# A macaron transformer kernel: the input's block sums move into the places of the lead tiles' weights, between the lead tiles' products

## The chip, the cores and the metric

The kernel runs on one core of one Trainium2 chip. The metric is the device time of one execution in microseconds (us), the median over several runs. A core has a matrix engine (TensorE, PE in the profile; PEld are its weight loads), a vector engine (VectorE, DVE), an activation engine (ScalarE, ACT), GpSimd (POOL) and SyncE (SP), which here issues the DMAs. Each engine works through its own queue in order and waits at semaphores for the others.

## What is computed

Two layers act on a latent stream of 512 tokens and a context stream of 256 tokens, width 1024. Each layer is a half-step feed-forward part (FFN), a mixer and a second half-step FFN. There are four FFNs, numbered 0 to 3 here as in the kernel (`fi`); FFN 3 has no context stream.

```python
def swiglu(h, w_gu, w_down):
    gate, up = jnp.split(h @ w_gu, 2, axis=-1)
    return (jax.nn.silu(gate) * up) @ w_down

def macaron_ffn(x, g, shift, scale, gate, w_gu, w_down):
    h = modulate(rms_norm(x, g), shift, scale)
    return x + 0.5 * gate * swiglu(h, w_gu, w_down)
```

The hidden width is 2816, which is 22 tiles of 128 columns.

## The kernel before, in words

**Numbers in two parts.** Every fp32 operand of a product is split into a high part, rounded by ACT (`ACT.copy`), and a low part, the difference, made by DVE. Each product is then three matmuls (`mm3`, lines 296 to 298): high by high, high by low, low by high. `hh` and `hl` hold the two parts of the normed input, eight tiles `kt` of 128 rows by all the tokens.

**An FFN.** Its 22 gate and up tiles come in two ways. The first three are the lead tiles (`lead`, L446): plain products over kt = 0 to 7, once for each of two streams of columns. In FFN 1 and 2 the first stream is the context (256 columns) and the second the latent (512); in FFN 3 they are the two halves of the latent, 256 columns each. The weights of the lead tiles are loaded and split while the stage before still runs (`lead_ffn`, L323): 12 pairs of tiles of 512 columns, 48 KB of each partition. After a stream's products, `activate` (L410) makes silu(gate) times up from PSUM: L414 on ACT, L415 on DVE, L416 on ACT, L417 on DVE, through one buffer `sg`. The other 19 tiles come from `gu_w` (L504), a product scheme with seven block products in place of eight: the input is cut in four blocks (rows TOP and BOT, columns H1 and H2), and the products need four block sums of the input, `tblk[0]` to `tblk[3]`, and sums of the weights (L509 to L514). `gu_w` runs its products in the order w11, s1 on `tblk[0]`, s2 on `tblk[1]`, s4, s3 on `tblk[2]`, w12, w22 on `tblk[3]`. The second of them that writes the bank `ox` (s2) needs the first one's result copied out first (`keep`, L536), into a buffer of the tag `t2`.

**The block sums.** `combos` (L467) makes all four sums once for each FFN, for four k each: DVE subtractions and additions (L479 to L481, for the last sum L501 and L502) into a `tsum` buffer of the tags `nacc` and `t2` (two buffers each), then the high part on ACT (L474) and the low part on DVE (L475). In FFN 1 to 3 it is called after `lead`, when the lead tiles' pool is closed (L571) and a pool for eight tiles of sums is opened in the same 48 KB (32 KB in FFN 3).

**After the lead tiles** come the down products of the first three hidden tiles (`down`, L609; residual at L309), then chunks of `gu_w` and `down` in turn. Weights stand in a ring of 6 slots (8 in FFN 3) filled by `fill` (ACT L317, DVE L318). DVE also makes the modulation rows of later stages (L146) in FFN 0 to 2.

**PSUM.** There are eight banks, four of the tag `ps` and four of `pb`. The second stream of the lead tiles holds six of them in FFN 1 and 2 and three in FFN 3 until `activate` has read them.

**Order.** The order on each engine is no written one: a scheduler sets it when the program is built, by program order and by when its own model has each instruction ready. A tile that takes the place of another waits for all that read the other.

Of the kernel before, what the change touches and what calls it, by code (L numbers as in the profile page):

```python
# [51 lines left out]
def hybrid_backbone_kernel(ctx: ExitStack, tc: tile.TileContext, A: dict, out: bass.AP):  # L52
# [69 lines left out]
    def pump(n=1):  # L122
        for _ in range(n):
            if pending:
                try:
                    next(pending[0])
                except StopIteration:
                    pending.pop(0)
# [194 lines left out]
    def lead_ffn(fi):  # L323

        lp, close = opened("lead%d" % fi, side="right")
        ws = [[tuple(lp.tile([P, 512], F32R, tag=q, name="lead" + q, bufs=12) for q in "hl") for _ in range(4)] for _ in range(3)]

        def load():
            for i in range(3):
                for w, a in zip(ws[i], wload(A["wgl"][fi, i], 2048, 4)):  # L330
                    fill(w, a, LEAD, act_last)
                yield
        return ws, close, load()

    def lead_mixer(src, name):

# [15 lines left out]
    def ffn(l, f, with_ctx, jobs=(), next_sub=None, opening=False, lead_in=None, lead_out=None):  # L352
# [9 lines left out]
        TOP, BOT = slice(0, 4), slice(4, 8)  # L362
        nslot = NSLOT if jobs else 8
        set_psum(f"pf{fi}", "single")
        pool_t = []
        with tc.tile_pool(name=f"ffn{fi}", bufs=1, reuse_waits="tile") as fp:

            def slot():
# [5 lines left out]
            def tt(dt=F32R):  # L374
                return pool_t[0].tile([P, 4 * nh], dt, tag="tt", name="tt", bufs=8)
# [23 lines left out]
            def lead_k(w):  # L399

                return [tuple(tuple(a[:, (kt % 2) * 256 + j * P:(kt % 2) * 256 + j * P + P] for a in w[kt // 2]) for j in range(2)) for kt in range(KT)]

            def act_tiles():
                return [fp.tile([P, T], F32R, tag="a" + q, name="a" + q, bufs=NACT) for q in "hl"]
# [41 lines left out]
            def lead(ws, each=None):  # L446

                acts = acts0
                for c0, n in (LAT, CT) if opening else (CT, LAT) if with_ctx else (LA, LB):
                    if n == S:  # L450
                        drain()
                    bs = [gate_up(n) for _ in ws]
                    for kt in range(KT):
                        if each is not None and n == S:
                            each(kt)
                        for w, b in zip(ws, bs):
                            for j in range(2):
                                down_last[:] = [mmg(b[j], w[kt][j], kt, c0, n, kt == 0 and (j == 0 or n == S), kt == KT - 1 and (j == 1 or n == S))]
                        pump()
                    for act, b in zip(acts, bs):  # L460
                        activate(act, c0, *b)
                drain()
                return acts

            tblk = []
            pe_last, dve_last = [], []

            def combos():

                def tmp(tag):  # L470
                    return sm.tile([P, 512], F32, tag=tag, name="tsum", bufs=2)[:, :nh]

                def done(i, k, t):
                    ACT.copy(tblk[i][0][:, k], t)  # L474
                    return V.tensor_tensor(tblk[i][1][:, k], t, tblk[i][0][:, k], op=ALU.subtract)  # L475

                def sums(e, o, first, *terms):
                    op = ALU.subtract
                    e.tensor_tensor(o, first[0], terms[0][0], op=op)  # L479
                    e.tensor_tensor(o, o, terms[0][1], op=op)  # L480
                    e.tensor_tensor(o, o, first[1], op=ALU.add)  # L481

                ts = [tt().rearrange("p (k c) -> p k c", k=4) for _ in range(8)]
                t1, t3, t2, t4 = (ts[2 * i:2 * i + 2] for i in range(4))
                tblk.extend((t1, t2, t3, t4))
                bl = [[[(hh[:, kt, q], hl[:, kt, q]) for q in (H1, H2)] for kt in (k, k + 4)] for k in range(4)]
                for k in range(4):
                    (b11, b12), (b21, b22) = bl[k]
                    a = tmp("nacc")
                    sums(V, a, b12, b11)  # L490
                    done(0, k, a)
                    b = tmp("t2")
                    sums(V, b, b22, b12)
                    done(2, k, b)
                for k in range(4):
                    (b11, b12), (b21, b22) = bl[k]
                    b = tmp("t2")
                    sums(V, b, b22, [x[:, k] for x in t1])
                    done(1, k, b)
                    a = tmp("nacc")  # L500
                    V.tensor_tensor(a, b21[0], b, op=ALU.subtract)  # L501
                    V.tensor_tensor(a, a, b21[1], op=ALU.add)  # L502
                    dve_last[:] = [done(3, k, a)]

            def gu_w(ft):
                a11, a21, a12, a22 = wload(A["wgs"][fi, ft - 3], 2048, 4)
# [55 lines left out]
            if opening:  # L562
                open_t()
                rows = [tt(F32) for _ in range(4)]
                ws = lead_slots()
                acts0 = [act_tiles() for _ in range(3)]
                queue = start_up(rows, ws, lead_k, fill, lead)
            else:
                acts0 = [act_tiles() for _ in range(3)]
                queue = lead([lead_k(w) for w in lead_in[0]])  # L570
                lead_in[1]()  # L571
                open_t()
            ndirect = NDIRECT[fi]
            if ndirect == 3:
                combos()
            ft = 3

            state = {}
# [15 lines left out]
            for ci, nf in enumerate(CHUNKS[fi > 0]):  # L594
                while len(queue) < nf:
                    queue.append((gu if ft < ndirect else gu_w)(ft))
                    ft += 1
                    if ft == ndirect:
                        combos()
                acts, queue = queue[:nf], queue[nf:]  # L600
                last = ci == len(CHUNKS[fi > 0]) - 1
                norms = {}
                if last:
                    some_jobs(len(jobs))
                if last and next_sub is not None:
                    sqrt_table()
                    sq = cycle([sg_tile()[:, :512], s3_tile()] + job_tiles(fp, 0) + [job_tiles(fp, 1) for _ in range(NWM)])
                    norms = {vec_index(q[0]): Norm(*q, *next_sub, room=lambda: next(sq), tail=TAIL) for q in (LAT, CT)}
                    pool_t[1]()  # L609
                    lead_next = lead_out()  # L610

                def down(dt, w, c0, n):
                    po = bank()
                    for i in range(nf):
                        cs = slice(i * P, i * P + P)
                        with issue_after(pe_last if i == 0 else ()):
                            down_last[:] = [mm3(po[:, :n], w[0][:, cs], w[1][:, cs], acts[i][0][:, c0:c0 + n], acts[i][1][:, c0:c0 + n], i == 0, i == nf - 1)]
                    dve_last[:] = [residual(po[:, :n], dt, c0, n, l, s)]
                    pump()
                    tick()  # L620
                    if norms:
                        nm = norms[vec_index(c0)]
                        nm.add(dt)
                        if dt == KT - 1:
                            pending.append(nm.steps(L0, L1) if c0 == 0 else nm.steps(W0, W1))
                    elif last:
                        nc.sync.dma_start(out[:, dt], st["x"][:, dt, :S])

                ws = []
                order = [(b, q) for b in range(KT) for q in (LAT, CT)]  # L630
                if last:
                    order = [(b, q) for q in (CT, LAT) for b in range(KT)]
                for b, q in order:
                    if q is CT and not with_ctx:
                        continue
                    if b == len(ws):
                        for r in wload(A["wdn%d_%d" % (min(fi, 1), ci)][max(fi - 1, 0), b // 4], 512 * nf, 4 if nf > 2 else 2):
                            w = put(r)
                            ws += [w] if nf > 2 else [[a[:, i * 256:(i + 1) * 256] for a in w] for i in range(2)]
                    down(b, ws[b], *q)  # L640
                    if norms and q is CT and b >= 4:
                        next(lead_next[2], None)
# [147 lines left out]
    def out_proj(att, wname, l, with_ctx, next_sub, close, fi):  # L790
# [4 lines left out]
            V.tensor_tensor(hl[:, k, :n], att[k][:, :n], hh[:, k, :n], op=ALU.subtract)  # L795
        close()
        set_psum("po%d" % l, "single")
        ws, close_lead, load = lead_ffn(fi)
        streams = (CT, LAT) if with_ctx else (LA, LB)
        lag = 3  # L800
        order = []
# [6 lines left out]
        with tc.tile_pool(name="outp%d" % l, bufs=1, reuse_waits="tile") as op:  # L808
# [15 lines left out]
                    next(load)  # L824
            for _ in load:
                pass
        return ws, close_lead


    def mixer_even(lead_in):  # L830
# [697 lines left out]
```

## Time and profile before

| | |
|---|---|
| median of three runs | 2727.33 us (2726.94 to 2730.42) |
| profiled execution | 2732.5 us, of which the span is 2730.7 us |
| PE busy | 2601.6 us, 95% |
| DVE busy | 2113.4 us, 77% |
| ACT busy | 1149.7 us, 42% |
| mean granted clock of TensorE | 0.979 of full speed |

The span is what the trace covers, from the first to the last instruction; times in the rows below count from its start. Busy times of PE hold pipelined matmuls, so the distance from one start to the next is the cost of a matmul in a row of many, not its duration. A row of the order of time has its start, its duration, engine, line, operation, what it writes and reads, and in brackets how long the engine sat idle before it and whose end released it.

### The profile page before, as it was taken

What the parts mean: (1) busy time and instruction counts of PE and PEld (TensorE: products, weight loads), DVE (VectorE), ACT (ScalarE), POOL (GpSimd) and SP (SyncE); (2) the same over time, 40 slices, a digit from 0 to 9 for tenths busy, and PEclk for the clock granted to TensorE, in tenths of its full rate; (3) what the DMA queues carried; (4) which work ended last, traced back from release to release, by engine and by line L of the source; (5) the groups of instructions that cost most, each with busy time, mean ns of one, the idle gap of its engine ahead of it and who ended that gap; (6) DMA issues with size and microseconds to landing.
All of it is one profiled execution on the core that took longest, in us unless ns stands there. A gap on an engine that the chain in (4) does not pass through costs nothing.

```text
span 2730.7 us, 41329 instructions
## 1 busy us (share of the span) xinstructions
PE 2601.6 (95%) x15826; PEld 2365.0 (87%) x15826; DVE 2113.4 (77%) x4506; ACT 1149.7 (42%) x2262; POOL 63.9 (2%) x43
## 2 busy tenths in 40 slices
PE   3999999999999999899999898999998999999999
PEld 2899999989877887899999887999998767989998
DVE  8999999982667657888889777777787467687877
ACT  3333343342445532334433524343435356444544
POOL 0000000000221000000000000000000000000000
PEclk9999999999999999899999999999999999999999
DMA  7334344341212320333333302323333100312232
GB/s 263 108 97 136 128 134 144 106 166 38 79 34 86 120 89 24 115 120 121 112 113 120 116 29 94 105 101 116 105 105 108 55 16 1 132 41 100 100 110 93
DMA packets 81167, 271.65 MB, mean 99 GB/s; under 512 B 11002, under 2 KB 15518, under 8 KB 66248
## 3 DMA queue, kind: packets, MB, share of 16 engines
q1 hardware_dynamic: 80408, 268.76, 29.3%
q8 instruction: 124, 2.03, 0.3%
q14 instruction: 75, 0.61, 0.1%
q0 software_dynamic: 560, 0.24, 0.0%
HBM read 262.35 MB, written 5.24 MB: 98 GB/s over the span
## 4 chain that ended last, share of the span: by engine, by line
PE 85%; DVE 9%; ACT 2%; DMA 2%; issue 1%; SPq 0%; DVEq 0%; ACTq 0%
PE ps L296 13%; PE ps L297 13%; PE ps L298 13%; PE pb L297 11%; PE pb L296 11%; PE pb L298 11%; PE pp L296 2%; PE pp L297 2%; PE pp L298 2%; PE ps L764 2%; DVE xn L309 1%; PE ps L1027 1%; PE pp L1293 1%; PE ps L1076 1%; PE ps L1329 1%
## 5 line engine op out<-in xcount | busy, mean ns | idle before, releaser
L317 ACT CAST wh<-wr 128x512 fp32r<-128x512 f32 (+1 forms) x672 | 391.6, 592 | 754.8 <-PE pb L297 258.3
L318 DVE TENSOR_TENSOR wl<-wr,wh 128x512 fp32r<-128x512 f32 (+1 forms) x672 | 434.2, 651 | 107.9 <-ACT wh L317 105.3
L146 DVE CUSTOM_DVE_ANT_0 junk<-wm,silc 128x512 bf16<-128x512 f32 x416 | 284.2, 683 | 6.8 <-DMA wm<-in_wmod 3.6
L296 PE MATMUL ps<-hh,wh 128*128 128x384 f32 (+2 forms) x728 | 249.6, 344 | 2.1 <-ACT wh L280 1.4
L298 PE MATMUL ps<-hh,wl 128*128 128x384 f32 (+2 forms) x728 | 246.9, 339 | 1.0 <-DVE wl L281 1.0
L297 PE MATMUL ps<-hl,wh 128*128 128x384 f32 (+2 forms) x728 | 247.2, 340 | 0.0
L296 PE MATMUL pb<-tt,wh 128*128 128x384 f32 (+2 forms) x600 | 196.6, 328 | 28.5 <-ACT u L536 28.5
L296 PE MATMUL ps<-ah,wh 128*128 128x512 f32 (+1 forms) x640 | 217.5, 347 | 1.8 <-DVE xn L309 1.2
L297 PE MATMUL ps<-al,wh 128*128 128x512 f32 (+1 forms) x640 | 218.9, 344 | 0.0
L298 PE MATMUL ps<-ah,wl 128*128 128x512 f32 (+1 forms) x640 | 218.3, 343 | 0.0
L296 PE MATMUL pb<-hh,wh 128*128 128x384 f32 (+2 forms) x632 | 204.4, 323 | 5.1 <-ACT hh L261 4.9
L297 PE MATMUL pb<-hl,wh 128*128 128x384 f32 (+2 forms) x632 | 203.6, 322 | 2.3 <-DVE hl L262 2.2
L298 PE MATMUL pb<-hh,wl 128*128 128x384 f32 (+2 forms) x632 | 203.1, 321 | 0.0
L297 PE MATMUL pb<-al,wh 128*128 128x512 f32 (+1 forms) x576 | 200.2, 349 | 0.0
L298 PE MATMUL pb<-ah,wl 128*128 128x512 f32 (+1 forms) x576 | 199.7, 348 | 0.0
L296 PE MATMUL ps<-tt,wh 128*128 128x384 f32 (+1 forms) x600 | 194.1, 324 | 5.4 <-ACT u L536 5.4
L297 PE MATMUL pb<-tt,wh 128*128 128x384 f32 (+2 forms) x600 | 196.8, 328 | 0.0
L298 PE MATMUL pb<-tt,wl 128*128 128x384 f32 (+2 forms) x600 | 196.7, 328 | 0.0
L296 PE MATMUL pb<-ah,wh 128*128 128x512 f32 (+1 forms) x576 | 195.9, 349 | 0.6 <-DVE xn L309 0.6
L298 PE MATMUL ps<-tt,wl 128*128 128x384 f32 (+1 forms) x600 | 194.5, 324 | 0.1
L297 PE MATMUL ps<-tt,wh 128*128 128x384 f32 (+1 forms) x600 | 194.5, 324 | 0.0
L309 DVE SCALAR_TENSOR_TENSOR xn<-ps,hgt,xn 128x512 f32<-128x512 f32 (+1 forms) x184 | 117.7, 644 | 45.6 <-PE ps L298 44.8
(348 smaller groups left out, 6349.2 us busy)
## 6 DMA issues: line engine op xcount, KB each, us to landing
wr<-in_wgs SPq DMA_DIRECT2D x76, 1024.0 KB
wm<-in_wmod SPq DMA_DIRECT2D x240, 256.0 KB
wr<-in_wdn SPq DMA_DIRECT2D x44, 768.0 KB
wr<-in_wdn SPq DMA_DIRECT2D x18, 512.0 KB
wr<-in_wgl SPq DMA_DIRECT2D x9, 1024.0 KB
wr<-in_wmod SPq DMA_DIRECT2D x16, 512.0 KB
wr<-in_wqk_ab SPq DMA_DIRECT2D x5, 1024.0 KB
bias<-in_bias_ab SPq DMA_DIRECT2D x12, 384.0 KB
```

Source lines behind the costliest of these rows:

```text
L146: V.tensor_tensor_reduce(junk, w, silc[v], 1.0, 0.0, ALU.mult, ALU.add, outs[v])
L296: PE.matmul(o, wh, rh, start=start, stop=False, skip_group_check=again)
L297: PE.matmul(o, wh, rl, start=False, stop=False, skip_group_check=again)
L298: return PE.matmul(o, wl, rh, start=False, stop=stop, skip_group_check=again)
L309: return V.scalar_tensor_tensor(xs, ps_ap, hgt[:, vec_index(c0), l * 3 + s, dt:dt + 1], xs, ALU.mult, ALU.add)
L317: ACT.copy(h[:, :n], src)
L318: eng.tensor_tensor(lo[:, :n], src, h[:, :n], op=ALU.subtract)
L764: PE.transpose(out=o[:, c * P:(c + 1) * P], in_=p[:, c * P:(c + 1) * P], identity=ident)
L1027: PE.matmul(ps[a][:, i * 256:i * 256 + 256], q[hs, q0:q0 + P], k[hs, k0:k0 + 256], start=i == 0 and n == 0, stop=i == 1 and n == 2)
L1076: PE.matmul(po[a * HD:a * HD + HD, j * P:(j + 1) * P], v[keys(a, j)[c]][:, vc[a]], pts[a][:, c], start=j == 0 and c == 0, stop=j == 3 and ...
L1293: PE.matmul(bs[a][:, k0:k0 + w], q[hs, qs], k[hs, k0:k0 + w], start=n == 0, stop=n == 2)
L1329: PE.matmul(keep[t][a * HD:a * HD + HD, j * P:(j + 1) * P], val[:, c, a * HD:a * HD + HD], pts[a][c], start=j == 0 and c == 0, stop=j == 3 ...
```

## The change

In `lead_ffn`, the weights of the lead tiles lie in four pairs of tiles of 1536 columns. Tile `a` of them holds what all three lead tiles need for kt = 2a and 2a + 1. `lead_ffn` also returns its pool, and this pool stays open through the FFN, in place of the separate pool for the sums.

`combos(i)` now makes one block sum. In FFN 1 to 3 it is called within the second stream of the lead tiles: sum 0 ahead of the products of kt = 2, sum 1 ahead of kt = 4, sum 2 ahead of kt = 6 and sum 3 after kt = 7, ahead of `activate`. Sum `i` takes the place of the weights of kt = 2i and 2i + 1. In FFN 0 (`opening`) the four calls stand where the one stood, and `tblk` is made in the order in which it is used. Sum 3 is now b21 minus the stored `tblk[1]` in three DVE operations, where it was made in two from the unsplit `tsum` of sum 1. The temporaries alternate between `nacc` and `t2` by k.

```diff
     def lead_ffn(fi):
         lp, close = opened("lead%d" % fi, side="right")
-        ws = [[tuple(lp.tile([P, 512], F32R, tag=q, name="lead" + q, bufs=12) for q in "hl") for _ in range(4)] for _ in range(3)]
+        wide = [[lp.tile([P, 1536], F32R, tag="%s%d" % (q, a), name="lead" + q) for q in "hl"] for a in range(4)]
+        ws = [[tuple(w[:, i * 512:(i + 1) * 512] for w in wide[a]) for a in range(4)] for i in range(3)]
...
-        return ws, close, load()
+        return ws, close, load(), lp
...
+                        if each is None and kt and kt % 2 == 0 and c0 == streams[1][0]:
+                            combos(kt // 2 - 1)
                         for w, b in zip(ws, bs):
...
+                    if each is None and c0 == streams[1][0]:
+                        combos(3)
                     for act, b in zip(acts, bs):
                         activate(act, c0, *b)
...
+            def combos(i):
+
+                if opening:
+                    t = [tt() for _ in range(2)]
+                else:
+                    t = [pool_t[0].tile([P, 1536], F32R, tag="%s%d" % (q, i), name="tt")[:, :4 * nh] for q in "hl"]
+                t = [a.rearrange("p (k c) -> p k c", k=4) for a in t]
+                tblk.append(t)
+                b11, b12, b21, b22 = ([a[:, k, q] for a in (hh, hl)] for k in (TOP, BOT) for q in (H1, H2))
+                first, second = ((b12, b11), (b22, tblk[0]), (b22, b12), (b21, tblk[min(i, 1)]))[i]
                 for k in range(4):
...
+                    o = sm.tile([P, 512], F32, tag=("nacc", "t2")[k % 2], name="tsum", bufs=2)[:, :nh]
+                    V.tensor_tensor(o, first[0][:, k], second[0][:, k], op=ALU.subtract)
+                    V.tensor_tensor(o, o, second[1][:, k], op=ALU.subtract)
+                    V.tensor_tensor(o, o, first[1][:, k], op=ALU.add)
+                    ACT.copy(t[0][:, k], o)
+                    dve_last[:] = [V.tensor_tensor(t[1][:, k], o, t[0][:, k], op=ALU.subtract)]
...
+                pool_t[:] = [lead_in[3] if len(lead_in) > 3 else lead_in[2], lead_in[1]]
                 queue = lead([lead_k(w) for w in lead_in[0]])
-                lead_in[1]()
-                open_t()
             ndirect = NDIRECT[fi]
-            if ndirect == 3:
-                combos()
...
-                    if ft == ndirect:
-                        combos()
+                    if opening and ft == ndirect:
+                        for i in range(4):
+                            combos(i)
```

## Rows read from the trace of the kernel before

**Rows 1.** Waits of PE, whole span: total us, times, longest us

```profile
PE pb L296 <- ACT u L536: 28.5, 3, 15.0
PE ps L296 <- ACT u L536: 5.4, 2, 4.3
```

**Rows 2.** PE in order of time, around the stalls of FFN 1, 2 and 3

```profile
1085.27 0.34 PE L298 MATMUL ps<-tt,wl 128*128 128x384 f32 x1
1100.60 0.69 PE L296 MATMUL pb<-tt,wh 128*128 128x384 f32 x1 [14.99 <-ACT u L536]
...
1106.53 0.46 PE L296 MATMUL ps<-hh,wh 128*128 128x384 f32 x1
...
1651.14 0.69 PE L296 MATMUL pb<-tt,wh 128*128 128x384 f32 x1 [12.27 <-ACT u L536]
...
1656.11 0.44 PE L296 MATMUL ps<-hh,wh 128*128 128x384 f32 x1
...
2405.82 0.50 PE L296 MATMUL ps<-ah,wh 128*128 128x512 f32 x1
...
2422.27 0.28 PE L296 MATMUL ps<-hh,wh 128*128 128x256 f32 x1
...
2425.03 0.27 PE L298 MATMUL pb<-tt,wl 128*128 128x256 f32 x1
2429.60 0.58 PE L296 MATMUL ps<-tt,wh 128*128 128x256 f32 x1 [4.30 <-ACT u L536]
...
2434.35 0.38 PE L297 MATMUL pb<-hl,wh 128*128 128x256 f32 x1
...
2443.79 0.39 PE L296 MATMUL pb<-tt,wh 128*128 128x256 f32 x1 [1.26 <-ACT u L536]
```

**Rows 3.** A stretch: length, busy us of PE, PEld, DVE, ACT, POOL; PEclk, DMA

```profile
1100.60:1106.60 6.00, 6.00 (x19) 6.00 (x20) 5.90 (x16) 2.50 (x5) 0.00 (x0) 0.50 0.15 51
```

**Rows 4.** ACT in order of time: the end of FFN 1's stall, an activation of FFN 3

```profile
1100.07 0.48 ACT L536 COPY u<-pb 128x384 f32<-128x384 f32 x1 [0.42 <-DVE tt L475]
...
2406.91 0.37 ACT L414 ACTIVATE sg<-ps 128x256 f32<-128x256 f32 x1
```

**Rows 5.** DVE in order of time: ends of its idle times, FFN 1, 2, 3

```profile
1053.61 0.69 DVE L415 TENSOR_TENSOR sg<-sg,ps 128x512 f32<-128x512 f32 x1 [15.25 <-PE ps L298]
...
1605.98 0.69 DVE L415 TENSOR_TENSOR sg<-sg,ps 128x512 f32<-128x512 f32 x1 [17.46 <-PE ps L298]
...
2404.91 0.42 DVE L415 TENSOR_TENSOR sg<-sg,pb 128x256 f32<-128x256 f32 x1 [7.09 <-ACT sg L414]
```

**Rows 6.** DVE in order of time: operations of the sums, FFN 1 and FFN 3

```profile
1059.27 0.55 DVE L475 TENSOR_TENSOR tt<-tsum,tt 128x384 fp32r<-128x384 f32 x1
1059.73 0.55 DVE L479 TENSOR_TENSOR tsum<-hh 128x384 f32<-128x384 f32 x1
...
2408.49 0.41 DVE L415 TENSOR_TENSOR sg<-sg,ps 128x256 f32<-128x256 f32 x1
2408.82 0.42 DVE L479 TENSOR_TENSOR tsum<-hh 128x256 f32<-128x256 f32 x1
```

**Rows 7.** PE in order of time, FFN 1: second stream, down products, first of `gu_w`

```profile
1022.54 0.39 PE L296 MATMUL pb<-hh,leadh 128*128 128x512 f32 x1
...
1056.13 0.28 PE L296 MATMUL ps<-ah,wh 128*128 128x256 f32 x1
...
1057.80 0.63 PE L296 MATMUL pb<-ah,wh 128*128 128x512 f32 x2
...
1081.22 0.34 PE L296 MATMUL pb<-hh,wh 128*128 128x384 f32 x1
```

**Rows 8.** DVE in order of time: before its idle, s2's low part, FFN 3's first residual

```profile
1037.80 0.56 DVE L481 TENSOR_TENSOR tsum<-tsum,hl 128x384 f32<-128x384 f32 x1
...
1081.99 0.68 DVE L318 TENSOR_TENSOR wl<-wr,wh 128x512 fp32r<-128x512 f32 x1
...
2419.30 0.75 DVE L309 SCALAR_TENSOR_TENSOR xn<-ps,hgt,xn 128x512 f32<-128x512 f32 x1
```

More of the change, by code (lines that the diff above doesn't have):

```diff
@@ L364, in ffn @@
         set_psum(f"pf{fi}", "single")
-        pool_t = []
+        pool_t, tblk = [], []
+        pe_last, dve_last = [], []
         with tc.tile_pool(name=f"ffn{fi}", bufs=1, reuse_waits="tile") as fp:
@@ L448, in lead @@
                 acts = acts0
-                for c0, n in (LAT, CT) if opening else (CT, LAT) if with_ctx else (LA, LB):
+                streams = (LAT, CT) if opening else (CT, LAT) if with_ctx else (LA, LB)
+                for c0, n in streams:
                     if n == S:
@@ L463, in lead @@
                 return acts
[L465 to L486, printed above, removed]
-                for k in range(4):
[L488 to L503, printed above, removed]
@@ L797, in out_proj @@
         set_psum("po%d" % l, "single")
-        ws, close_lead, load = lead_ffn(fi)
+        ws, close_lead, load, lp = lead_ffn(fi)
         streams = (CT, LAT) if with_ctx else (LA, LB)
@@ L826, in out_proj @@
                 pass
-        return ws, close_lead
+        return ws, close_lead, lp
     def mixer_even(lead_in):
```

## The prediction

> **What bounds the kernel now.** Read the page first: PE is busy for 95% of the span, so only stretches in which it stands still can be won without fewer matmuls. The waits of PE name them [rows 1]: "pb" and "ps" matmuls wait 28.5 and 5.4 us for the copy of L536. Read next the order of time on PE [rows 2]: four of these waits stand at the start of `gu_w`, after its second product: 14.99 us in FFN 1, 12.27 in FFN 2, 4.30 and 1.26 in FFN 3, together 32.8 us (the other 1.1 us lie later and the change doesn't touch them). The copy itself takes 0.5 us. It waited for a DVE operation of the block sums, L475 [rows 4]: its buffer has the tag `t2`, which the sums' temporaries use too, so the second product on `ox` waits for the last sums. The reader is to see that it is DVE's making of the sums that is late, not ACT.
>
> Each of the three long stalls costs more than itself, since the clock falls: after the first the granted clock is 0.50 of full speed, 1.2 GHz, for six us [rows 3]. In FFN 1, 18 matmuls start between 1100.60 and 1106.53, 5.93 us; at the distance of 0.176 us that they have before (23 steps from 1081.22 to 1085.27 [rows 2, 7]) they would take 3.2, so 2.8 us are lost. In FFN 2 15 steps take 4.97 us instead of 2.6, 2.3 lost. In FFN 3 19 steps take 4.75 instead of 2.3 (0.12 each, from 2422.27 to 2425.03), 2.5 lost [rows 2]. After the 1.26 us the distances stay short. All in all 32.8 + 7.6 = 40.4 us hang on the late sums.
>
> The last view is DVE's order of time: while PE works on the second stream of the lead tiles, DVE stands idle for 15.25 us, 17.46 us and 7.09 us [rows 5]. It has the first temporaries ready and no place to put the sums, because the lead weights hold it.
>
> **Part by part.** *The place.* With the weights laid out by kt, the place of sum i is free once kt = 2i + 1 is through. In FFN 1 the second stream runs from 1022.54 to 1056.13, 33.6 us or 4.2 per kt [rows 7], so the places come free at about 1031, 1039, 1048 and 1056. The input tiles that the sums read are written before that: DVE's last work ahead of its idle time, the twelfth operation of the sums in this stretch, starts at 1037.80, behind the last input tile [rows 8].
>
> *The sums.* A sum is now 16 DVE operations at 0.46 us from start to start, 7.4 us, in FFN 1 and 2, and at 0.33 us, 5.3 us, in FFN 3 [rows 6]. A place comes free every 8.4 us in FFN 1, so sums 0 to 2, 48 operations, fit beside the products: 12 already run there, and 36, or 16.6 us, go into the idle 15.25 to 17.46 us. In FFN 3 the idle 7.09 us take only some 21 more; about 31, sums 2 and 3, come after the stream. Sum 3, 7.4 us, follows from 1056 and lies beside the down products, which last until 1081.22 [rows 7]; its users and the `t2` buffers come after that. So in FFN 1 and 2 the sums should be ready some 10 us early, where they were 15 late.
>
> *Four added operations a FFN* (sum 3 reads the stored parts): 4 x 0.46 = 1.8 us of DVE, hidden as above in FFN 1 and 2. In FFN 0, whose stage shows no wait for the sums, they are hidden by the matmuls in front of its first `gu_w`; without that cover they would cost 1.8 us. From "nothing" to 1.8; I take nothing.
>
> *What is late next: the activations.* Sum 2's end and sum 3 now compete with L415 and L417 just when the second stream ends; before, DVE was idle there. How long does a ready operation wait? In FFN 3 the second activation was through on ACT at 2407.28 and L415 started at 2408.49 [rows 4, 6]: 1.2 us, about four operations of sums, which is how many the four temporaries keep in flight. I read that as DVE serving ready work in turn. So L415 and L417 may each be late by 4 x 0.46 = 1.8 us, 3.7 us together. In FFN 1 and 2 context downs cover the first 1.7 us (1056.13 to 1057.80 [rows 7]): 0 to 2 us a FFN, I take 1. In FFN 3 the first down product starts at 2405.82 [rows 2], 0.5 us after L415 ends [rows 5], without cover: 0 to 2.7 us (two times 4 x 0.33), I take 2, nearer the upper end since there DVE is full with sums 2 and 3.
>
> *Then the weights of s2.* In FFN 1 their low part is written by 1082.7 [rows 8] while s2 could start at 1085.45: on time even with all sums in the way, and earlier without. In FFN 3 the residuals start at 2419.30 [rows 8], eight of at most 0.75 us, then w11's and s1's low parts, a weight sum and s2's low part, four of at most 0.68: 8.7 us, to 2428.0, while s2 needs its low part at about 2425.4. Lower bound 0 (weights served between residuals), upper 2.6; I take 1.5. Stalls of this size didn't drop the clock in the last row of [rows 2].
>
> *DMAs.* None is added or moved; the loads of `gu_w`'s weights wait for their staging buffers as before, and those are released sooner. The rows of modulation (L146) that ran during the stalls now run beside products; each FFN has the same number, and FFN 1's later chunks carry the same rate without a wait of PE, so I cost them at nothing, up to 1 us if they push a weight.
>
> **Sum.** FFN 1: 14.99 + 2.8 - 1 = 16.8. FFN 2: 12.27 + 2.3 - 1 = 13.6. FFN 3: 4.30 + 1.26 + 2.5 - 2 - 1.5 = 4.6. Together 35 us. The profiled execution took 2732.5 us (span 2730.7), so it would take 2697.5; it stands 5.2 us above the median, so the median should go from 2727.3 to about 2692. With all the taken costs at their lower ends the gain is 40.4 (2687), at their upper ends 40.4 - 4 - 5.3 - 1.8 - 1 = 28.3 (2699).
>
> **Rivals.** *The banks starve.* In program order sum 3 stands ahead of `activate`. If the scheduler keeps to that order instead of serving in turn, sums 2 and 3 fill DVE until about 1056 + 7.4 = 1063 in FFN 1, and six of the eight banks stay held. Two are left; PE can do one context down (1.05 us) and part of a latent one and then waits some 5 us, with the 2.5 us of slow clock that the three stalls show: 7.5 us in each of FFN 1 and 2. In FFN 3 sums 2 and 3 take 10.6 us from 2404.9, and the down products need the activation at once: 8 us and the clock, 10.5. The gain is 40.4 - 25.5 = 15, so 2712. For it: the place in the program. Against it: before, sums stood ahead of the residuals and the modulation rows too, and were served among them. The Trainium skill (Perfetto Trace Analysis, Matmuls) wants independent groups of matmuls to rotate through the banks so that the reading out of one overlaps the products of the next; by that rule this is where the change hurts, and no row of before shows such a wait.
>
> *Taking turns, slower than before.* The sums now live in the pool of the weights that are being read. If a product of kt = 2i had to wait for sum i - 1 (the build waiting for a whole pool or a whole tag in place of a tile, or ACT held by a copy that waits for its place while an input tile stands behind it), PE and DVE would alternate: three sums of 7.4 us in each of FFN 1 and 2 and of 5.3 us in FFN 3, 22 + 22 + 16 = 60 us lost for 35 won, 2752. It decides against the change from 12 us lost a FFN on. Against it: products from kt = 2i on read other tiles, and the input tiles are written by 1037.80 [rows 8] while kt = 7 needs the last only at about 1052.
>
> *It doesn't do what it says.* If the places are released only at the end of the stream, the sums start at 1056 as before and the time stays within 5 us of 2727.
>
> *More is won.* The activations find gaps, FFN 3 gets its weights on time, and DVE's work ahead of the first chunk saves another small wait: 2680 to 2686.
>
> **How the numbers follow.** Forecast 0.62 (2686 to 2699), banks starve wholly or in part 0.18 (2699 to 2714), no effect 0.06, taking turns 0.08, more won 0.06. The range 2682 to 2714 holds the first two and most of the last. A measurement here can tell about 0.2%, 5.5 us: faster 0.62 + 0.18 + 0.06 + 0.01 = 0.87; same 0.06, slower 0.07 (of the eight hundredths for taking turns one is a mild case that is still faster).
>
> **What would show it.** Right: no wait of PE for L536 over 2 us at the start of `gu_w` in FFN 1 and 2; DVE without idle time over 5 us in the second streams; L474 and L475 between lead products; PEclk at 1.00 from the lead tiles to the second chunk. FFN 3 should keep a wait of 1 to 3 us, at its first down product or at s2. Wrong: waits of `ps` or `pb` matmuls for L415 or the residual right after the lead tiles (banks), waits of lead products for `hh` or for DVE (turns), or the old stall in its old place.

## The result, and the profile after

The changed kernel takes 2693.95 us (median of four runs, 2693.27 to 2694.98) against 2728.51 for the kernel before beside it: a ratio of 0.987, 95% interval 0.986 to 0.988, or 34.6 us. The forecast was 35 us and 2692. Its profiled execution took 2693.69 us (span 2691.9), with a mean granted clock of 0.987 where before had 0.979.

The waits of PE over the whole span of the changed kernel (total us, times, longest us); L521 is the copy that was L536, L418 and L419 belong to `activate`. These answer to [rows 1]:

```profile
PE pb L296 <- ACT u L521: 1.6, 1, 1.6
PE ps L298 <- DVE wl L318: 1.4, 1, 1.4
PE ps L296 <- ACT u L521: 1.3, 2, 1.1
...
PE pb L296 <- ACT ah L418: 0.9, 1, 0.9
```

The 28.5 and 5.4 us for the copy are now 1.6 and 1.3, and 1.1 of the latter is the late wait that was there before.

The gain is read best from windows, stretches of the trace. Columns: window, length, busy us of PE, PEld, DVE, ACT and POOL, then granted clock, DMA share, GB/s. First the kernel before: the second stream of FFN 1, then in FFN 1, 2 and 3 the first three `gu_w`, from the first matmul of `gu_w` to the next down product:

```profile
1022.50:1056.10 33.60, 33.60 (x146) 27.03 (x145) 17.20 (x32) 7.75 (x14) 0.00 (x0) 1.00 0.00 0
...
1081.22:1143.69 62.47, 47.48 (x254) 47.16 (x253) 55.26 (x122) 27.51 (x54) 0.00 (x0) 0.86 0.30 97
1634.47:1693.78 59.31, 47.04 (x255) 46.71 (x253) 46.33 (x92) 27.41 (x54) 0.00 (x0) 0.88 0.26 86
2422.27:2461.06 38.79, 33.15 (x254) 32.31 (x252) 35.73 (x72) 23.05 (x53) 0.00 (x0) 0.91 0.28 96
...
2429.60:2434.60 5.00, 4.92 (x21) 4.61 (x22) 4.65 (x10) 3.94 (x9) 0.00 (x0) 0.50 0.01 2
```

The last row is the stretch behind FFN 3's first stall.

The same stretches of the changed kernel, and between them FFN 2's and FFN 3's down products ahead of `gu_w`:

```profile
1018.26:1051.86 33.60, 33.60 (x147) 27.00 (x146) 33.32 (x69) 13.38 (x26) 0.00 (x0) 1.00 0.00 1
...
1076.91:1121.37 44.46, 44.46 (x254) 44.46 (x253) 40.93 (x91) 23.02 (x46) 0.00 (x0) 1.00 0.41 134
1586.72:1613.67 26.95, 25.89 (x146) 22.01 (x145) 25.39 (x52) 8.31 (x16) 0.00 (x0) 1.00 0.21 69
1613.67:1658.12 44.45, 44.45 (x254) 44.45 (x253) 33.46 (x66) 22.42 (x45) 0.00 (x0) 1.00 0.34 109
2370.70:2387.35 16.65, 16.65 (x73) 13.54 (x73) 14.62 (x40) 5.73 (x14) 0.00 (x0) 1.00 0.01 2
2387.35:2422.28 34.93, 31.53 (x254) 30.45 (x252) 31.44 (x60) 21.58 (x49) 0.00 (x0) 1.00 0.31 106
```

Two things are to be seen. In the second stream PE does the same 33.60 us of work, but DVE works 33.32 us of them where it worked 17.20: its idle time is filled. And the `gu_w` stretches shrink by 62.47 - 44.46 = 18.0, 59.31 - 44.45 = 14.9 and 38.79 - 34.93 = 3.9 us. PE's busy time falls by 3.0, 2.6 and 1.6 us, the rest are waits. In FFN 1 and 2 the fall is what the slow clock had cost. In FFN 3 that was 2.5 us (the granted clock is 0.50 from 2429.60 on, and 19 steps take 4.75 us in place of 2.3 [rows 2]). The changed kernel gives 0.9 of it back, since PE stops more often there and its first steps after each stop are long: from 2390.48 to 2392.41 below, two steps of 0.12 take 0.50 us besides the wait.

The low parts of the sums (L488, once L475) and of the activation in DVE's order of time in the changed kernel, FFN 1. The second stream runs from 1018.26 to 1051.86, so the places come free at about 1027, 1035, 1043 and 1052:

```profile
1033.07 1.02 DVE L488 TENSOR_TENSOR tt<-tsum,tt 128x384 fp32r<-128x384 f32 x2
...
1042.91 0.54 DVE L488 TENSOR_TENSOR tt<-tsum,tt 128x384 fp32r<-128x384 f32 x1
...
1051.34 0.55 DVE L488 TENSOR_TENSOR tt<-tsum,tt 128x384 fp32r<-128x384 f32 x1
1052.28 0.68 DVE L419 TENSOR_TENSOR al<-sg,ah 128x512 fp32r<-128x512 f32 x1
...
1062.65 0.55 DVE L488 TENSOR_TENSOR tt<-tsum,tt 128x384 fp32r<-128x384 f32 x1
```

Sum 0 is stored by 1036, sum 1 by 1043.5, sum 2 by 1051.9, and the last part of sum 3 at 1063.2. The first product that reads a sum starts at 1079.03.

What PE still waits for, in its order of time; these answer to [rows 2]:

```profile
1599.99 1.20 PE L296 MATMUL pb<-ah,wh 128*128 128x512 f32 x4 [0.89 <-ACT ah L418]
1601.35 0.50 PE L297 MATMUL pb<-al,wh 128*128 128x512 f32 x1 [0.16 <-DVE al L419]
...
2390.48 0.28 PE L297 MATMUL ps<-tt,wh 128*128 128x256 f32 x1
2392.19 0.39 PE L298 MATMUL ps<-tt,wl 128*128 128x256 f32 x1 [1.43 <-DVE wl L318]
2392.41 0.28 PE L296 MATMUL ps<-tt,wh 128*128 128x256 f32 x1
...
2394.29 0.39 PE L298 MATMUL pb<-hh,wl 128*128 128x256 f32 x1 [0.23 <-DVE wl L318]
...
2395.92 0.38 PE L296 MATMUL ps<-tt,wh 128*128 128x256 f32 x1 [0.18 <-ACT u L521]
...
2405.01 0.38 PE L296 MATMUL pb<-tt,wh 128*128 128x256 f32 x1 [1.57 <-ACT u L521]
```

FFN 1 has none, FFN 2 waits 1.05 us for late activations, and FFN 3 keeps 1.84 us in its first `gu_w` (low parts of weights, 0.18 for a copy) and 1.57 in its second.

### The profile page after: what moved, and what is told of

The parts are those of the page before. It is cut to its first block, busy times and chain, and to the rows that moved or that the text cites. A ratio compares the mean times of both kernels' runs of the same rounds, so it can differ in the third digit from the quotient of the medians.

```text
span 2691.9 us, 41363 instructions
## 1 busy us (share of the span) xinstructions
PE 2591.4 (96%) x15826; PEld 2354.3 (87%) x15826; DVE 2119.7 (79%) x4522; ACT 1149.6 (43%) x2262; POOL 62.9 (2%) x43
## 4 chain that ended last, share of the span: by engine, by line
PE 88%; DVE 7%; ACT 2%; issue 1%; DMA 1%; SPq 0%; DVEq 0%; ACTq 0%
PE ps L296 13%; PE ps L297 13%; PE ps L298 13%; PE pb L297 12%; PE pb L296 12%; PE pb L298 12%; PE pp L296 2%; PE pp L297 2%; PE pp L298 2%; PE ps L747 2%; PE ps L1010 1%; PE pp L1276 1%; PE ps L1059 1%; DVE xn L309 1%; PE ps L1312 1%
## 5 line engine op out<-in xcount | busy, mean ns | idle before, releaser
L309 DVE SCALAR_TENSOR_TENSOR xn<-ps,hgt,xn 128x512 f32<-128x512 f32 (+1 forms) x184 | 117.7, 644 | 45.7 <-PE ps L298 44.8
```

The costliest lines, as they stand in the source:

```text
L309: return V.scalar_tensor_tensor(xs, ps_ap, hgt[:, vec_index(c0), l * 3 + s, dt:dt + 1], xs, ALU.mult, ALU.add)
```

## The experiments

The kernel before ran beside each group of experiments on the same chip; its medians are 2728.2 us (e1 to e4), 2727.0 (e5 to e8), 2729.2 (e9, e10) and 2726.5 (e11, e12). Differences below are taken from the changed kernel's 2693.95 or from the median of the kernel before in the same group.

### Is it the place, or the calls between the products? (e1, e10)

```diff
-                        if each is None and kt and kt % 2 == 0 and c0 == streams[1][0]:
-                            combos(kt // 2 - 1)
...
                 queue = lead([lead_k(w) for w in lead_in[0]])
+                for i in range(4):
+                    combos(i)
```

> The changed kernel with the places still freed kt by kt, but all four block sums called behind the lead tiles' products and activations, as in the kernel before. Theory that the place is what counts: the order of an engine was made by readiness in the kernel before too (twelve operations of the sums ran there ahead of the activations that stand before them in the program), so the sums still go into the second stream, no wait for the x1 copy over 2 us, 2692 to 2700 us. Rival, that it is the calls between the products that count: the sums start behind the stream as before and the stalls of 15, 12 and 4 us stay, 2722 to 2730 us.

Measured: 2692.4 us (2691.76 to 2694.21). In the stretches around the three FFNs the waits of PE are those of the changed kernel to 0.01 us, and DVE and ACT have the same operations in the same order. So the calls between the products bring nothing by themselves: the scheduler sets the order by when an operation can run, and what decides is when the place comes free.

e10 moves the call of sum 3 behind the activations:

> The changed kernel with sum 3 called behind the activations of the second stream in place of ahead of them. Theory that turns decide and not the place in the program (as e1 says for all four sums): the same order comes out, the 0.89 and 0.16 us that the down products wait in FFN 2 stay, 2692 to 2695 us. Rival, that the activations then go first: these waits go, and sum 3 has slack to spare, 2690 to 2693 us; if sum 3 comes late for it, longer than 2695.

Measured: 2694.62 us (2694.47 to 2696.13). The order is that of the changed kernel on every engine, so the waits in FFN 2 stay. e1, the changed kernel and e10, all three with one order, measure 2692.4, 2693.95 and 2694.62 us: medians of one order differ by up to 2.2 us here.

### The same tiles, free in the wrong order (e5, e6, e7)

```diff
-  tag="%s%d" % (q, i)
+  tag="%s%d" % (q, 3 - i)
```

with the calls as in e1, which keeps the changed kernel's order and time, so that only the index differs; e6 does it in FFN 1 alone, e7 in FFN 3 alone.

> e1 with the places given out backwards in FFN 1, 2 and 3: sum i takes the tile of lead weights 3 - i, so the place of sum 0 is free only when the second stream is through, that of sum 3 first; the same tiles, sums and number of operations. Theory that a place free kt by kt, in the order of the sums, is the cause: the sums start behind the stream, the three stalls come back as long as in e3 (18.6, 15.6 and 6.9 us, with the clock), 2728 to 2738 us. Rival, that it is enough that no pool is closed and opened between (the pool's own bookkeeping was late): 2692 to 2700 us.

> The same backwards places in FFN 1 alone, FFN 2 and 3 as in the changed kernel. The share of FFN 1: my sum has 16.8 us for it, with the added operations now uncovered up to 21: 2710 to 2716 us, with a stall of 15 to 19 us at the start of gu_w in FFN 1 and none in FFN 2. Rival, that the win of one FFN is given back in the next stage (a time to which later work is bound, a DMA): under 2705 us.

> The same backwards places in FFN 3 alone. The share of FFN 3: my sum has 4.6 us for it (8.1 us of stalls and clock, less 2 for late activations and 1.5 for late weights), e3's stall was 2.6 us longer than before's: 2697 to 2702 us. Rival, that FFN 3 won nothing since the sums only got in the way of its activations and weights: 2692 to 2696 us.

Measured: 2736.56, 2714.88 and 2701.15 us, that is 42.6, 20.9 and 7.2 us over the changed kernel; all three as expected by my theory (e5 and e7 in the upper part of their ranges). In e5 DVE's idle time in FFN 1 is back (line numbers are one higher here; DVE's order of time):

```profile
1048.21 0.69 DVE L418 TENSOR_TENSOR sg<-sg,ps 128x512 f32<-128x512 f32 x1 [15.17 <-PE ps L299]
```

and with it the stall, in PE's order of time:

```profile
1098.96 0.69 PE L297 MATMUL pb<-tt,wh 128*128 128x384 f32 x1 [18.65 <-ACT u L522]
```

An idle time of 15.17 us on DVE turns into a wait of 18.65 us on PE some 50 us later, by an index alone. e6 and e7 show that the gain of an FFN stays where it is won: e6 has 18.60 us of stall in FFN 1, none in `gu_w` of FFN 2, and ends 20.9 us later.

### Is it the ring, or the order? (e2, e3, e4)

e2 gives x1 and x5 of the kernel before (the copies of the results of w11 and s1) a ring of two buffers of their own; e3 makes the sums of the kernel before in the order of their use, 0 to 3, in the old place (in FFN 0 too); e4 does both.

```diff
-  x1 = keep("t2", ox)
-  x5 = keep("t2", oc)
+  x1 = keep("x", ox)
+  x5 = keep("x", oc)
```

> The kernel before, its x1 and x5 copied to a ring of their own in place of t2, nothing else changed. Rival theory, that the sums were in time and only the shared buffers of t2 made the x1 copy wait: the stalls vanish, 2690 to 2700 us. My theory: the second product on ox (s2) reads tblk[1], whose last part the old order makes as third last of all parts, about when the copy got its buffer (1099.5 in FFN 1), so the same stall stands in front of or within s2, 0 to 2 us shorter a FFN: 2721 to 2729 us.

> The kernel before with the sums in the order of their use (sum 0, 1, 2, 3, four added operations a FFN), in the old place behind the lead tiles, x1 and x5 on t2. Theory that the order is what counts: tblk[1] is ready by about 1076 in FFN 1 and the stalls go, 2695 to 2705 us. My theory: the x1 copy still stands behind the last sum's temporaries in the ring of t2, and there are 4 x 0.46 us more of them, so the stalls stay and are up to 2 us longer: 2726 to 2736 us.

> The kernel before with both: sums in the order of use and x1, x5 in a ring of their own, in the old place. Then s1 and s2 wait for sums 0 and 1 alone, s3 for sum 2, w22 for sum 3. Theory that order and ring together are the whole cause: 2692 to 2700 us. My theory: DVE's 60 operations are late as a whole, sums 2 and 3 come some 8 and 15 us behind sum 1, so about half the stall remains, now in front of s3 and w22: 2708 to 2722 us.

Measured: e2 2728.07 us (ratio to before 1.000, interval 0.999 to 1.001), e3 2734.61 (6.4 us slower, interval 0.18 to 0.40%), e4 2726.99 (0.9999, interval 0.9989 to 1.0008). e2 came as my theory said. e3's time did too, but its stalls grew by more than the up to 2 us that it gave. In e2, PE in FFN 1, and at its end in FFN 3:

```profile
1087.16 0.44 PE L297 MATMUL pb<-tt,wh 128*128 128x384 f32 x1 [1.08 <-DVE tt L475]
...
1098.31 0.69 PE L296 MATMUL pb<-tt,wh 128*128 128x384 f32 x1 [8.98 <-ACT tt L474]
...
2441.62 0.39 PE L296 MATMUL pb<-tt,wh 128*128 128x256 f32 x1 [1.26 <-ACT x L536]
```

The ring was only where the lateness became visible: without it the same product waits for the parts of sum 1 themselves in FFN 1 and 2. In FFN 3 it waits for the two parts of its weights instead (3.54 us for ACT's, 1.13 for DVE's), which are late there too. The last row matters below: FFN 3's 1.26 us are still there with a ring that the sums don't use, so they don't hang on that ring.

In e3 the one stall of FFN 1 is 18.60 us, 3.6 longer than before, for four added operations of 0.46 us: on the path such an operation costs about twice its own time.

e4 is a miss of mine: 2708 to 2722 us was expected. PE in FFN 1:

```profile
1084.05 0.44 PE L298 MATMUL pb<-tt,wl 128*128 128x384 f32 x1 [0.96 <-DVE wl L318]
...
1087.79 0.44 PE L296 MATMUL ps<-hh,wh 128*128 128x384 f32 x1 [1.71 <-ACT wh L317]
...
1090.69 0.64 PE L298 MATMUL ps<-hh,wl 128*128 128x384 f32 x1 [2.29 <-DVE wl L318]
...
1099.24 0.69 PE L296 MATMUL pb<-tt,wh 128*128 128x384 f32 x1 [5.03 <-ACT u L514]
```

One stall of 15 us became four of 10 us together, for weights that DVE is as late with as with the sums, and for the copy of u2, which stands on ACT behind copies of the sums and takes a buffer of `nacc`, a ring that they use too. The stretch of the three `gu_w` is 59.29 us long against 62.47 before and 44.46 in the changed kernel; PE is busy for 49.30 us of it, 4.8 more than in the changed kernel. In two stretches with work for PE, 3.50 and 5.20 us long, the granted clock is half, which is some 4.3 us lost, so the several stalls cost more clock than the one:

```profile
1090.69:1094.19 3.50, 3.50 (x10) 3.01 (x10) 3.50 (x8) 0.00 (x0) 0.00 (x0) 0.51 0.22 75
1099.24:1104.44 5.20, 5.20 (x16) 5.20 (x17) 5.20 (x11) 2.57 (x5) 0.00 (x0) 0.50 0.18 50
```

The three stretches gain 3.2 + 2.6 - 1.0 us, and the medians don't show even that. Neither ring nor order helped while DVE started the work too late.

### How much room is there? (e8, e9)

```diff
-                for k in range(4):
+                for k in list(range(4)) * (3 if i == 3 and not opening else 1):
```

makes sum 3 three times over (e8), or with 2 twice (e9).

> The changed kernel with sum 3 made three times over (the same values again): 32 added DVE operations in each of FFN 1, 2 and 3, 14.8 us in FFN 1 and 2 and 10.6 in FFN 3. My theory, that the sums are ready some 10 us early in FFN 1 and 2: most is hidden there, 0 to 6 us each, and FFN 3, where DVE has only 1.9 us without work before the residuals, pays 6 to 10 with the clock: 2700 to 2715 us. Rival, that the change only just makes it and DVE's time is the bound of these stretches: all of it shows, 40 us and the clock, 2735 us or more.

> The changed kernel with sum 3 made twice: 16 added DVE operations a FFN, 7.4 us of DVE in FFN 1 and 2, 5.3 in FFN 3. e8 cost all of its 40 us: there the last part of FFN 1's sums ended at 1093.0 in place of 1063.2, 30 us later for 14.8 us of work, since behind the stream the sums get every second turn of DVE. Theory that there is slack, but that an operation added behind the stream costs double: the sums end at about 1078 in FFN 1, before the x1 copy at 1080, so FFN 1 and 2 pay 0 to 2 us each and FFN 3, without slack, 5 to 8: 2699 to 2706 us. Rival, that there is no slack and DVE is the bound of these stretches: 20 us in all and the clock, 2714 to 2722 us.

Measured: e8 2737.16 us, e9 2700.56. e8 is a miss: my theory said 2700 to 2715, the rival 2735 or more, and the time is the rival's. More than the gain is gone, though 32 operations are 14.8 us in FFN 1 and the sums were ready 16 us ahead of their use. PE in e8, FFN 1, where it waits for a residual and for the x1 copy:

```profile
1067.76 0.50 PE L296 MATMUL pb<-ah,wh 128*128 128x512 f32 x1 [0.43 <-DVE xn L309]
...
1093.67 0.69 PE L296 MATMUL pb<-tt,wh 128*128 128x384 f32 x1 [11.51 <-ACT u L521]
```

The last part of a sum in DVE's order:

```profile
1094.10 0.55 DVE L488 TENSOR_TENSOR tt<-tsum,tt 128x384 fp32r<-128x384 f32 x1
```

It ends at 1094.65. Counted from the end of the second stream (1051.86 in the changed kernel, 1050.41 in e8) the sums end after 44.2 us instead of 11.3: 33 us later for 14.8 us of work. Once the stream is through, residuals, activations, weights and modulation rows take every second turn of DVE, which has no idle time there: 45 of its 93 operations in these 44.2 us are the sums'. Still there is room, which e9 shows (2700.56 us is in the range of its theory), again with its last part of a sum in FFN 1:

```profile
1079.51 0.57 DVE L488 TENSOR_TENSOR tt<-tsum,tt 128x384 fp32r<-128x384 f32 x1
```

It ends at 1080.08, 27.2 us behind the stream (which ends at 1052.92 here), 16 us later for 7.4 us of work, and that is in time. What PE waits for in e9, FFN 1 and FFN 3:

```profile
1067.26 0.50 PE L297 MATMUL pb<-al,wh 128*128 128x512 f32 x1 [1.10 <-DVE al L419]
...
1070.27 0.49 PE L296 MATMUL pb<-ah,wh 128*128 128x512 f32 x1 [0.41 <-DVE xn L309]
...
2397.93 0.58 PE L296 MATMUL ps<-tt,wh 128*128 128x256 f32 x1 [8.13 <-ACT u L521]
```

No product of FFN 1 or 2 waits for a sum; FFN 3, without room, waits 8.13 us. So the margin of the changed kernel in FFN 1 and 2 lies between 7.4 and 14.8 us of DVE's work. The waits of 0.43 and 0.41 us for a residual (L309) are waits for a bank.

### Can FFN 3's rest be won? (e11, e12)

e11 has nine slots in FFN 3 in place of eight; e12 lays the first four split weights of `gu_w` into the thirds of the lead tiles that FFN 3's sums don't use.

> The changed kernel with nine slots for split weights in FFN 3 in place of eight. In the changed kernel ACT's first copy for gu_w (w11) starts at 2384.14, released by the down products that read the slot until then. Theory that FFN 3's wait of 1.43 us for the low part of s2 comes from the slots: w11's copy goes early, and s1, s2 follow one place sooner: 0.5 to 2 us less, 2692 to 2694 us. Rival, that it is DVE's turns (residuals and weights taking turns): no change, 2693 to 2695 us.

> The changed kernel where FFN 3's first gu_w puts w11, s1, s2 and s4 into the third of each lead weight tile that the sums leave empty there (256 of 384 columns are used), so that they wait for no slot. Theory that the slots make s2 late: its copy and low part come before the residuals, the waits of 1.43 and 0.23 us go, 2690 to 2693 us. Rival, that DVE's time is the limit in FFN 3 (as e8 and e9 show for added sums): four low parts and three weight sums, some 4 us, push the activations or the last sum by as much, 2694 to 2698 us.

Measured: 2693.20 us (2692.05 to 2696.76) and 2694.23 (2693.78 to 2695.58): no change that these medians can tell. In e11 the first three `gu_w` of FFN 3 wait 3.3 us (0.98, 0.23, 0.18, 1.49, 0.39) where the changed kernel has 3.4. In e12, PE:

```profile
2371.86 0.50 PE L296 MATMUL ps<-ah,wh 128*128 128x512 f32 x1 [0.90 <-ACT ah L419]
...
2403.99 0.39 PE L296 MATMUL ps<-hh,wh 128*128 128x256 f32 x1 [0.83 <-ACT u L525]
...
2413.70 0.38 PE L296 MATMUL ps<-tt,wh 128*128 128x256 f32 x1 [0.89 <-ACT u L525]
```

The waits for s2 and s4 are gone, as its theory said, but 0.90 us, for a late activation, stand in front of the first down product, and 1.7 for copies stand later. On balance FFN 3 gains up to there: the three `gu_w` take 32.23 us in place of 34.93, the lead and down products before them 1.1 more. But at 2672.41 a wait of 1.09 us for a copy stands in e12, which the changed kernel doesn't have, and takes most of the 1.6 back. No version found here beats the changed kernel by more than the measurement tells.

## Why the prediction was right, step by step

| | forecast, us | measured in the trace, us |
|---|---|---|
| FFN 1: stall and clock | 14.99 + 2.8 | 18.0 (clock 3.0) |
| FFN 1: activations late | -1 | 0 |
| FFN 2: stall and clock | 12.27 + 2.3 | 14.9 (clock 2.6) |
| FFN 2: activations late | -1 | -1.0 (down products 25.96 to 26.95) |
| FFN 3: stalls and clock | 4.30 + 1.26 + 2.5 | 4.30 + 2.5 |
| FFN 3: second `gu_w` | none left | 1.57 where 1.26 was: -0.3 |
| FFN 3: long first steps after PE's stops | no term | -0.9 |
| FFN 3: activations late | -2 | -0.2 |
| FFN 3: weights of s2 late | -1.5 | -1.8 (1.43 for s2, 0.23 for s4, 0.18 for a copy) |
| sum | 35.0 | 35.5 |

*The cause* was named rightly and is shown, by e1 and e5: the time at which a place comes free decides, not where the sums are called, nor (e2 to e4) the ring in which the stall is seen, nor the order of making. The Trainium skill (Perfetto Trace Analysis, Optimization Strategy) says that a gap repeating on the engine that should be saturated can mean that there is no room for the next tile. The runs agree that room was missing, with one addition: the gap on PE, 15 to 19 us in FFN 1, stands some 50 us behind the 15 us of DVE's idle time from which it comes, and only the latter shows the missing room.

*FFN 1 and 2* came within 1.2 and 0.3 us. The steps were: a place every 8.4 us, sums 0 to 2 beside the products, sum 3 beside the down products. The low parts at 1033, 1042.91 and 1051.34 show the first, the end at 1063.2 the second. "Ready some 10 us early" was 16 us in FFN 1 (1063.2 to 1079.03). But that isn't 16 us of room in DVE's work, as e8 had to teach: behind the stream each us of sums needs two. The signs that I had given came as well: DVE's longest idle time in the second streams is 2.34 us, in FFN 2.

*The activations.* The price by turns holds in FFN 2 as a sum, 1.05 us of waits where I took 1, though not in its parts (up to 1.8 us each): there the high part of the second activation ended at 1592.34 and its low part ran at 1595.35, three us later, which held up the third, for which PE waited. Of the 1.0 us by which these down products grew only 0.44 are longer waits, since before they had one of 0.61 us for a bank; the rest are PE's first steps after its stops. In FFN 1 none of it reaches PE. In FFN 3, where I took 2 us as nearer the upper end, the first down product doesn't wait at all. The step that failed is that DVE, full with sums, would serve the first activation late: at the end of the stream it was served at once.

*FFN 3's sum* of 4.6 against 3.7 is made of errors that cancel in part, which is luck: 1.26 us too much was to be won, 0.9 for the first steps after PE's stops had no term, 0.3 each came on top in the second `gu_w` and the weights, and 1.8 too much was paid for activations. The 1.26 us didn't go with the late sums: in the changed kernel 1.57 us stand there, and ACT's order of time shows why:

```profile
2402.21 0.62 ACT L317 CAST wh<-s 128x512 fp32r<-128x512 f32 x1
2402.73 1.65 ACT L317 CAST wh<-wr 128x512 fp32r<-128x512 f32 x3
...
2404.60 0.36 ACT L521 COPY u<-pb 128x256 f32<-128x256 f32 x1
```

ACT works without a pause, and the copy stands behind four weights and the high part of an activation. It is shorter or gone where PE comes later: 0.45 us behind a first stall of 6.86 (e7), none behind 6.85 to 8.13 (e3, e5, e9). The mistake was to read all four rows for L536 as one cause since they name one line; only the first three had a copy that waited. The clock term was right, 2.5 us. The weights of s2 were sized well, 1.43 us where I took 1.5, and the reason given holds: DVE takes residuals and weights in turn.

*Four added operations a FFN* cost nothing in FFN 1 and 2, as taken (e9: 16 more still don't reach a sum's reader). In FFN 0 too no product waits for a sum. Without cover they cost more than the 1.8 us that I gave: 3.6 us of stall in e3's FFN 1.

*The rivals.* The banks didn't starve: in these stretches of the changed kernel no product waits for a residual, and in FFN 1 a first wait of 0.41 us comes with 16 operations more. My sentence that no row of before shows such a wait was wrong, though; in FFN 2's down products there is one, and none in the changed kernel's:

```profile
1624.46 0.50 PE L296 MATMUL pb<-ah,wh 128*128 128x512 f32 x1 [0.61 <-DVE xn L309]
```

Products and sums didn't take turns: the second stream takes 33.60 us in both kernels. That nothing happens is what e5 shows when the places come free too late.

*The rest.* The two profiled spans lie 38.8 us apart, 3.3 more than the table. FFN 1's first `gu_w` already starts 4.3 us earlier (1081.22 and 1076.91), and stretches between the FFNs give back about 1. That start is 1081.22 and 1081.52 in the kernels with the old FFN 0 (before, e2) and 1075.9 to 1078.6 in e1, e3 to e7 and e10 to e12, which make FFN 0's sums in the new order, so part of it may belong to the change. But 2.9 of the 4.3 us lie behind FFN 0, in the mixer and up to the second stream: the same matmuls take 322.56 us (699.98 to 1022.54) before and 319.70 (698.56 to 1018.26) in the changed kernel, at a mean granted clock of 0.98 and 0.99. e10, with the changed kernel's order, took 321.49 there at 0.98, and e3, which has the new FFN 0, 322.41 at 0.98: this stretch varies from run to run. The median gain of 34.6 doesn't show the 3.3 us either; what is left of them stays open.

## What to carry to other kernels

Behind a stall of the engine that bounds the kernel look for idle time of its supplier well before it: here the work was hindered only by a missing place, and it was enough to make the place free piece by piece, in the order in which it is needed. Where the order was set by readiness, moving a call did nothing (e1, e10); moving the time at which its buffer comes free did all. Cost an operation by the stretch that it falls into: here once in the supplier's idle time, about twice where other work shared its turns. A stop of PE cost more than its wait, in the first steps behind it, even where the clock stayed at 1.00.

## What the runs showed that was not expected

The loss by the slow clock didn't grow with the stall. After 4.30 us without work the clock was 0.50 for some 5 us of work in the kernel before, 2.5 lost; after 8.13 us in e9, half speed lasted some 3 us, 1.6 lost. Windows of e9 in FFN 3, the stall and what follows it:

```profile
2389.80:2398.00 8.20, 0.07 (x2) 0.07 (x1) 8.13 (x17) 4.29 (x9) 0.00 (x0) 0.78 0.00 0
2398.00:2402.00 4.00, 4.00 (x22) 4.00 (x23) 3.94 (x7) 1.89 (x4) 0.00 (x0) 0.60 0.64 209
2402.00:2406.00 4.00, 4.00 (x36) 4.00 (x35) 3.56 (x8) 2.86 (x6) 0.00 (x0) 1.00 0.13 53
```

And ten us of stalls in four pieces (e4, some 4.3 us of clock) cost more of it than fifteen in one (3.0), while 1.43 and 1.57 us in the changed kernel's FFN 3 left the granted clock of the stretch at 1.00.
